# Sixteen row sums of layer 2's gate moved from beside layer 2's output projection to beside layer 1's

## The chip, the cores and the metric

One core of one Trainium2 chip. The metric is device time in microseconds (us) of the whole program, the median of several runs. Engines are named as in the profile: PE is TensorE's matmuls (PEld its weight loads), DVE is VectorE, ACT ScalarE, POOL GpSimd, SP SyncE, whose queue (SPq) issues nearly all DMA loads, in order.

## The reference

A two-layer decoder trunk on 512 tokens of width 2048. Layer 1 mixes tokens by retention (8 heads), layer 2 by latent attention. Each layer is modulated by the conditioning vector c:

```python
c_act = jax.nn.silu(c)
for i in range(DEPTH):
    mod = (c_act @ ada_w[i] + ada_b[i])[:, None, :]
    shift, scale, gate = jnp.split(mod, 3, axis=-1)
    h = rmsnorm(x, norm_g[i]) * (1.0 + scale) + shift
    ...                       # y = retention_branch(h, ...) or mla_branch(h, ...)
    x = x + gate * y
return rmsnorm(x, final_norm_g)
```

All is float32. `ada_w[i]` is 2048 x 6144, so shift, scale and gate have 2048 values each, and each value is a dot product of one row of the transposed matrix with silu(c), 2048 long. The gate of layer 2 is used only where layer 2's output projection is added to x.

## The kernel before

Matrix products run on PE as three passes with a high and a low part of each operand. ACT casts a float32 weight to its high part (L135), DVE subtracts to get the low part (L136); in the trace these are `o_p<-o_r` for layer 1's output projection.

**The row sums.** A modulation piece `(layer, section, part)` is 1024 values: section 0 is the shift, 1 the scale, 2 the gate, part 0 or 1 a half of 2048. The kernel computes a piece as 16 sums: for each of 8 blocks of 128 rows (`b`) and each half `j` of the 2048 products, a load of 128x1024 floats (512 KB, L1165, on SP) and one DVE instruction that multiplies by silu(c) and sums along the row (L1170). When a piece's last sum is through, `use_modulation` adds the halves and the bias: some small DVE operations (L1187 and L253 to L257). 96 such sums, six pieces, run beside layer 1's matmuls, on the list `later_rows`. In the part of layer 1 that matters here the loads' tiles carry the tag `odd0` with two buffers, so a load waits for the sum that used its buffer, two sums before.

**The steps.** Layer 1 is a list of `Step` objects, each one or two units of weights and their matmuls, with pieces of retention put beside them. A step has a count `rows`. At the end of step i, as many row loads as step i+1 has rows are issued on SP; their sums are written in step i+1, behind its other DVE work (`fetched`, `use_ended`). Within an engine the program's order is the order of execution.

**Layer 1's output projection** is four rounds, n = 0 to 3, one for each pair of heads; each of the rounds 0 to 2 has 16 steps: four columns of 512 outputs (`r`), and four units of weights in each (L1472 loads a unit, L1486 is its product, 24 matmuls of 128x512). Between two columns the sums in PSUM are copied out, and the next column's banks are seeded with earlier sums (L1437 and L1434, ACT). Beside round n the retention of heads 2n+2 and 2n+3 is computed, the even head from step 0, the odd one from step 4: rotation of q and k, scores, split of the values (`split_v`), values (y, L158 to L160), group norm (L1320 to L1332), gate (L1338), transposes (L1345). The last round has 8 such steps and then others. In the trace rounds 0, 1 and 2 lie at about 997 to 1109, 1109 to 1222 and 1222 to 1334 us, the last part up to about 1430 us. `light` says how many rows each step of a block has:

```python
light(block, (0, 0, 2, 3, 4, 6, 6, 7, 9, 9, 11, 11, 12, 13, 13, 15))
```

so step 13 of each of the three rounds has two rows.

**The gate of layer 2.** Its first half (part 0) is summed in layer 2's attention steps, two sums a step (`gate_load`, `gate_sum`). Its second half is summed beside layer 2's output projection (L2450, about 1925 us to the end): `o2_hooks(i)` is called at each of its units, and from i = 5 on it issues one load and writes the sum of the load before.

Of the kernel before, what the change touches and what calls it, by code (L numbers as in the profile page):

```python
# [9 lines left out]
F32 = mybir.dt.float32  # L10
# [6 lines left out]
P = 128  # L17
T = 512
NT = T // P
D = 2048  # L20
# [29 lines left out]
def hybrid_trunk_kernel(  # L50
# [32 lines left out]
    base = ctx.enter_context(tc.tile_pool(name="base", bufs=1))  # L83
# [11 lines left out]
    def big(name, dt=F32R):  # L95
        return base.tile([P, 2, T], dt, tag="big", bufs=16, name=name)
# [16 lines left out]
    def small(name, n=1):  # L113
        return base.tile([P, n], F32, tag="small", bufs=24, name=name)
# [135 lines left out]
    def modulate(i, ps_shift, ps_scale, k0, n):  # L250

        if ps_shift is not None:
            DVE.tensor_add(b_col[i][:, k0 : k0 + n], ps_shift, bias_c[i][:, k0 : k0 + n])  # L253
        if ps_scale is not None:
            s = small(f"mod{i}_{k0}", n)
            DVE.tensor_add(s, ps_scale, bias_c[i][:, KD + k0 : KD + k0 + n])
            return DVE.scalar_tensor_tensor(  # L257
                out=a_col[i][:, k0 : k0 + n], in0=s, scalar=1.0,
                in1=norm_c[i][:, k0 : k0 + n], op0=ALU.add, op1=ALU.mult,
            )  # L260
# [199 lines left out]
    A_, V_, T_, S_ = (getattr(mybir.EngineType, e) for e in ("Activation", "DVE", "PE", "SP"))  # L460

    @contextmanager
    def behind(*engines):

        with ExitStack() as stack:
            for e in engines:
                ins = next((i for i in reversed(nc.cur_bb.bb.instructions) if i.engine == e), None)
                if ins is not None:
                    stack.enter_context(tc.issue_after(ins))
            yield  # L470

    def queued(fn, *args):
        with behind(A_, V_, T_, S_):
            return fn(*args)
# [664 lines left out]
    for h in range(1, RH):  # L1139
        if h == 1:  # L1140
# [4 lines left out]
                sums=lambda u: {0: 2, 1: 3, 2: 4, 4: 5, 5: 6, 6: 7}.get(u),  # L1145
# [3 lines left out]
        steps += heads_steps(h)  # L1149


    row_pieces = [(0, 2, 0), (0, 2, 1), (1, 0, 0), (1, 0, 1), (1, 1, 0), (1, 1, 1)]
    later_rows = [(piece, b, j) for piece in row_pieces for b in range(8) for j in range(2)]
    row_sums, ended = {}, []

# [29 lines left out]
    def use_modulation(i, sect, part, mc):  # L1185
        both = small(f"mod_{i}_{sect}_{part}_s", 8)
        DVE.tensor_add(both, mc[:, 0, :], mc[:, 1, :])  # L1187
        if sect == 2:
            cols = slice(part * 8, part * 8 + 8)
            DVE.tensor_add(gate_c[i][:, cols], both, gate_bias[i][:, cols])  # L1190
        else:
            modulate(i, both if sect == 0 else None, both if sect == 1 else None, part * 8, 8)
# [205 lines left out]
    def light(block, which):  # L1398

        for i in which:  # L1400
            block[i].rows += 1

    block = []
# [113 lines left out]
    def go_on(n, r, after):  # L1517

        def done(t):
            if after is None:  # L1520
                o1_banks[n + 1, r, t] = o1_banks[n, r, t]
                return
            keep_sums(n, r, t)
            seed(n, after, t)

        return done

    for n in range(3):
        block = []
        cols = range(4) if n % 2 == 0 else range(3, -1, -1)  # L1530
        for r, after in zip(cols, [*cols[1:], None]):
            block += round_steps(n, r, go_on(n, r, after))
        heads += [retention(2 * n + 2 + i, big) for i in range(2)]
        light(block, (0, 0, 2, 3, 4, 6, 6, 7, 9, 9, 11, 11, 12, 13, 13, 15))
        steps += block


# [1 line left out]
    def outs(r, blocks, half=None):  # L1539

        late = None
        for b in blocks:
            add = x1_out(r, b, half)
            if late is not None:
                late()
            late = add
        late()

    block = round_steps(3, 3, lambda b: None) + round_steps(3, 2, lambda b: None)
    light(block, (0, 0, 2, 2, 4, 5, 6, 6))  # L1550
    block[3].follow = lambda: outs(3, range(4))

    def second_out():
# [169 lines left out]
    def l2_tile(tag, bufs, name, shape=(P, T), dt=F32):  # L1723
        return pools["l2"].tile(list(shape), dt, tag=tag, bufs=bufs, name=name)
# [412 lines left out]


    gate_c_half = {}
    gate_sums = [base.tile([P, 2, 8], F32, tag="mod_c", bufs=2, name=f"gate_sums{i}") for i in range(2)]  # L2140

    def gate_load(part, n):

        j, b = n // 8, n % 8
        if b == 0:
            half = gate_c_half[j] = big(f"c_gate{part}{j}", F32)
            nc.sync.dma_start(
                half.rearrange("p a n -> p (a n)"),
                c_d[0:1, j * 1024 : (j + 1) * 1024].rearrange("o n -> (o n)").partition_broadcast(P),
            )  # L2150
        aw = l2_tile("bw", 2, f"mod_gate_{part}{b}{j}", (P, 2, T))
        r0 = 2 * D + (8 * part + b) * P
        nc.sync.dma_start(aw, ada_t[1, r0 : r0 + P, j * 1024 : (j + 1) * 1024].rearrange("p (a n) -> p a n", a=2))
        return aw, part, j, b, gate_c_half[j]

    def gate_sum(aw, part, j, b, c_half):
        DVE.scalar_tensor_tensor(
            out=aw, in0=aw, scalar=1.0, in1=c_half, op0=ALU.mult, op1=ALU.mult,
            accum_out=gate_sums[part][:, j, b : b + 1],
        )  # L2160
        if (j, b) == (1, 7):
            use_modulation(1, 2, part, gate_sums[part])

    def attention_step(pr):

        nx = pr + 1
        here = [attend(2 * pr + s) for s in range(2)] if pr >= 0 else ()
        both = heads2[nx] = {}
        units_ahead()
        with behind(S_):  # L2170
            sums = [gate_load(0, 2 * nx + i) for i in range(2)]
        if here:
            (sc0, ex0, no0, tr0, sp0, lg0, va0, re0), (sc1, ex1, no1, tr1, sp1, lg1, va1, re1) = here
            queued(lg0)
            queued(lg1)
        low = next_unit("ukv")
        if here:
            for i in range(NT):
                queued(sc0, i)
            for i in range(NT):  # L2180
                queued(ex0, i)
        low()
        if here:
            no0()
        queued(uq_products, nx, 2)
        if here:
            for i in range(NT):
                queued(sc1, i)
            for i in range(NT):
                queued(ex1, i)  # L2190
        t1 = queued(rope_own, both["uq", 2], f"qr_{nx}")
        low = next_unit("ukv") if here else lambda: None
        if here:
            no1()
        low()
        for b in range(2):
            queued(uq_products, nx, b)
        sw = queued(rope_swap, both["uq", 2], f"qr_{nx}")
        low = queued(part_pair, nx, "uq", 0)
        queued(rope_turn, t1, sw)  # L2200
        queued(low)
        low = queued(part_pair, nx, "uq", 1)
        if here:
            queued(tr0)
        queued(low)
        lows = [queued(sp0, j) for j in range(3)] if here else []
        both["qr"] = big(f"qr_{nx}")
        queued(rope_highs, t1, both["qr"])
        for low in lows:
            queued(low)  # L2210
        queued(rope_lows, t1, both["qr"])
        for b in range(2):
            queued(uk_products, nx, b)
            low = queued(part_pair, nx, "uk", b)
            low_w = next_unit("uq")
            queued(low)
            low_w()
        if here:
            queued(va0)
            queued(re0)  # L2220
            queued(tr1)
            for low in [queued(sp1, j) for j in range(3)]:
                queued(low)
        for j in range(2):
            queued(uv_products, nx, j, (1,))
        for j in range(2):
            queued(uv_products, nx, j, (0, 2, 3))
            queued(gate_sum, *sums[j])
            queued(queued(part_values, nx, j))
        if here:  # L2230
            queued(va1)
            queued(re1)
# [130 lines left out]
    o2_in, o2_res = {}, {}  # L2363
    N_ENDS = 5

    gate_pending, gate_n = [], [0, 0]

    def o2_hooks(i):
        l2_hooks.get(i, lambda: None)()
        with behind(V_):  # L2370
            while gate_pending:
                gate_sum(*gate_pending.pop())
        with behind(S_):
            for _ in range(min(1, 16 - gate_n[0]) if 4 < i and i > gate_n[1] else 0):
                gate_pending.insert(0, gate_load(1, gate_n[0]))
                gate_n[0] += 1
        gate_n[1] = i

    def o2_parts(r, u):
        if u not in o2_in:  # L2380
# [235 lines left out]
```

## Time and profile before

| | |
|---|---|
| time, 3 runs | 2119.68, 2119.76 and 2120.03 us, median 2119.76 |
| span of the profiled execution | 2118.4 us |
| mean granted clock of PE | 0.999 |
| busy share of PE, DVE, ACT, POOL | 99%, 79%, 50%, 5% |
| bytes moved | 462.95 MB, 219 GB/s |
| sums of L1170 in layer 1's output projection | x56, 1219 ns busy each, 15.3 us of DVE idle ahead of them for their loads |

The execution that was profiled has a span 1.4 us below the median time. Rows of a timeline begin with the start in us from the start of the span, then the duration, the engine, the line, the operation and its tiles (output <- inputs); in brackets stands how long the engine was idle before and for whom it waited. A row of waits reads: the engine that waited, its tile and line, for whom, then us in total, the number of times and the longest. A matmul's duration overlaps that of the next; from start to start it is about 0.23 us for 128x512.

### The profile page before, as it was taken

What the parts mean: (1) busy time and instruction counts of PE and PEld (TensorE: products, weight loads), DVE (VectorE), ACT (ScalarE), POOL (GpSimd) and SP (SyncE); (2) the same over time, 40 slices, a digit from 0 to 9 for tenths busy, and PEclk for the clock granted to TensorE, in tenths of its full rate; (3) what the DMA queues carried; (4) which work ended last, traced back from release to release, by engine and by line L of the source; (5) the groups of instructions that cost most, each with busy time, mean ns of one, the idle gap of its engine ahead of it and who ended that gap; (6) DMA issues with size and microseconds to landing.
All of it is one profiled execution on the core that took longest, in us unless ns stands there. A gap on an engine that the chain in (4) does not pass through costs nothing.

```text
span 2118.4 us, 30062 instructions
## 1 busy us (share of the span) xinstructions
PE 2104.0 (99%) x11124; PEld 1812.6 (86%) x11124; DVE 1676.0 (79%) x2506; ACT 1055.5 (50%) x1622; POOL 103.6 (5%) x176
## 2 busy tenths in 40 slices
PE   8999999999999999999999999999999999999998
PEld 6888898989889888888888888898889989888888
DVE  7899888888888789666777778768978788886665
ACT  6765444444454444434344444345446575664443
POOL 1001010000000000000000000010001000000000
PEclk9999999999999999999999999999999999999999
DMA  9975786868787778856657556753566644346643
GB/s 381 406 280 195 248 276 222 283 211 272 239 263 250 242 229 283 265 172 196 222 173 241 201 198 230 258 191 108 164 189 209 190 129 149 118 137 219 222 142 138
DMA packets 230101, 462.95 MB, mean 219 GB/s; under 512 B 20881, under 2 KB 84401, under 8 KB 226369
## 3 DMA queue, kind: packets, MB, share of 16 engines
q1 hardware_dynamic: 217312, 421.07, 60.3%
q0 software_dynamic: 11920, 38.91, 4.7%
q8 instruction: 87, 1.43, 0.3%
q10 hardware_dynamic: 722, 1.06, 0.2%
q14 instruction: 60, 0.49, 0.1%
HBM read 417.96 MB, written 43.00 MB: 218 GB/s over the span
## 4 chain that ended last, share of the span: by engine, by line
PE 96%; DMA 1%; DVE 1%; ACT 0%; issue 0%; SPq 0%; DVEq 0%
PE o L1486 16%; PE o L2450 4%; PE x L884 2%; PE x L883 2%; PE x L885 2%; PE y L885 2%; PE y L884 2%; PE s L885 2%; PE s L884 2%; PE s L883 2%; PE y L883 2%; PE uv L2046 2%; PE qk L158 2%; PE s_qk L984 2%; PE x_qk L984 2%; PE qk L160 2%
## 5 line engine op out<-in xcount | busy, mean ns | idle before, releaser
L1486 PE MATMUL o<-o_h,o_p 128*128 128x512 f32 (+1 forms) x1088 | 323.0, 378 | 0.0
L1486 PEld LDWEIGHTS o<-o_h,o_p 128*128 128x128 f32 x1088 | 200.2, 188 | 37.1
L1486 PE MATMUL o<-o_l,o_p 128*128 128x512 f32 (+1 forms) x544 | 204.8, 376 | 0.0
L136 DVE TENSOR_TENSOR o_p<-o_r,o_p 128x1024 fp32r<-128x1024 f32 x64 | 78.1, 1222 | 54.3 <-ACT o_p L135 54.1
L1486 PEld LDWEIGHTS o<-o_l,o_p 128*128 128x128 f32 x544 | 102.3, 188 | 18.3
L2450 PE MATMUL o<-o_h,o_w 128*128 128x512 f32 (+1 forms) x336 | 82.7, 337 | 0.0
L1170 DVE SCALAR_TENSOR_TENSOR mod<-mod,c_odd 128x1024 f32<-128x1024 f32 x56 | 67.2, 1219 | 15.3 <-DMA mod<-in_ada_t_dram 15.3
L135 ACT CAST o_p<-o_r 128x1024 fp32r<-128x1024 f32 x64 | 66.7, 1054 | 22.4 <-PE o L1486 13.3
L158 PE MATMUL qk<-hT,qk_p 128*128 128x512 f32 x192 | 75.0, 391 | 0.0
L160 PE MATMUL qk<-hT,qk_p 128*128 128x512 f32 x192 | 74.9, 390 | 0.0
L389 DVE SCALAR_TENSOR_TENSOR aw<-aw,c_all 128x2048 f32<-128x2048 f32 (+1 forms) x37 | 73.2, 1997 | 2.1 <-DMA aw<-in_ada_t_dram 2.1
L159 PE MATMUL qk<-hT,qk_p 128*128 128x512 f32 x192 | 74.7, 389 | 0.0
L2450 PEld LDWEIGHTS o<-o_h,o_w 128*128 128x128 f32 x336 | 57.7, 188 | 6.9
L2450 PE MATMUL o<-o_l,o_w 128*128 128x512 f32 (+1 forms) x168 | 56.5, 337 | 0.0
L136 DVE TENSOR_TENSOR o_l<-o_in,o_h 128x1024 fp32r<-128x1024 f32 x24 | 29.3, 1222 | 34.2 <-ACT o_h L135 34.2
L1332 ACT ACTIVATE yn<-y,nmr,gn_r 128x512 f32<-128x512 f32 x32 | 22.3, 778 | 67.7 <-DVE nmr L1326 67.7
L135 ACT CAST o_h<-o_in 128x1024 fp32r<-128x1024 f32 x24 | 25.3, 1052 | 61.6 <-PE o L159 40.5
L158 PE MATMUL o<-o_h,o_w 128*128 128x512 f32 x128 | 50.1, 391 | 0.0
L160 PE MATMUL o<-o_h,o_w 128*128 128x512 f32 x128 | 49.8, 389 | 0.0
L159 PE MATMUL o<-o_l,o_w 128*128 128x512 f32 x128 | 49.8, 389 | 0.0
L1170 DVE SCALAR_TENSOR_TENSOR mod<-mod,c_bm 128x1024 f32<-128x1024 f32 x40 | 48.7, 1219 | 0.0
L448 PE MATMUL g<-hT,g_p 128*128 128x512 f32 x192 | 46.1, 389 | 0.0
(1532 smaller groups left out, 6238.3 us busy)
## 6 DMA issues: line engine op xcount, KB each, us to landing
mod<-in_ada_t_dram SPq DMA_DIRECT2D x96, 512.0 KB, 5.7
o_r<-in_ret_w_out_dram SPq DMA_DIRECT2D x64, 512.0 KB, 5.5
aw<-in_ada_t_dram SPq DMA_DIRECT2D x28, 1024.0 KB, 9.5
mod_gate<-in_ada_t_dram SPq DMA_DIRECT2D x32, 512.0 KB, 4.4
o_w_raw<-in_mla_w_out_dram SPq DMA_DIRECT2D x32, 512.0 KB, 4.4
qk_r<-in_ret_w_in_dram SPq DMA_DIRECT2D x48, 256.0 KB, 3.5
qk_r<-qk_d SPq DMA_DIRECT2D x32, 256.0 KB, 6.1
v_r<-v_d SPq DMA_DIRECT2D x32, 256.0 KB, 5.7
```

The lines of the kernel that those rows point to most:

```text
L135: ACT.copy(hi, src)
L136: DVE.tensor_sub(lo, src, hi.bitcast(F32))
L158: PE.matmul(o, lhs[0], rhs[0], start=first and not seeded, stop=False, skip_group_check=seeded)
L159: PE.matmul(o, lhs[0], rhs[1], start=False, stop=False, skip_group_check=seeded)
L160: return PE.matmul(o, lhs[1], rhs[0], start=False, stop=last, skip_group_check=seeded)
L883: PE.matmul(banks[b], a[0], w[0], start=first, stop=False, skip_group_check=True)
L884: PE.matmul(banks[b], a[0], w[1], start=False, stop=False, skip_group_check=True)
L885: PE.matmul(banks[b], a[1], w[0], start=False, stop=True, skip_group_check=True)
L984: PE.matmul(o, w[wp][:, i, b * P : (b + 1) * P], a[ap], start=first and i + b + k == 0, stop=k == 2, skip_group_check=True,)
L1170: DVE.scalar_tensor_tensor(out=aw, in0=aw, scalar=1.0, in1=silu_c[j], op0=ALU.mult, op1=ALU.mult, accum_out=row_sums[piece][:, j, b : b + 1],)
L1486: PE.matmul(o, w[i][:, ki, c0 + b * P : c0 + (b + 1) * P], a[j], start=first and i + j == 0, stop=last and i == 1, skip_group_check=True,)
L2450: PE.matmul(banks2[b][:, cols], w[0][i][:, 0, b * P : (b + 1) * P], o2_moving(w, u, cols)[j], start=u + i + j == 0, stop=u == KD - 1 and i ...
```

## The change

A seventh piece, `(1, 2, 1)`, the second half of layer 2's gate, is added to the list of pieces that are summed beside layer 1, and the steps of layer 1's output projection get 16 rows more: 4 in round 0, 5 in round 1, 6 in round 2, one in the last part. The loads and sums beside layer 2's output projection are taken out, and with them the two broadcast loads of silu(c) for that half (`c_gate10`, `c_gate11`). Since the list is worked through in order, each piece is finished some steps earlier than before, and its small operations move with it.

```diff
-    row_pieces = [(0, 2, 0), (0, 2, 1), (1, 0, 0), (1, 0, 1), (1, 1, 0), (1, 1, 1)]
+    row_pieces = [(0, 2, 0), (0, 2, 1), (1, 0, 0), (1, 0, 1), (1, 1, 0), (1, 1, 1), (1, 2, 1)]
...
+    more_rows = ((3, 8, 8, 13), (3, 4, 8, 9, 13), (2, 5, 8, 8, 10, 13))
     for n in range(3):
...
-        light(block, (0, 0, 2, 3, 4, 6, 6, 7, 9, 9, 11, 11, 12, 13, 13, 15))
+        light(block, (0, 0, 2, 3, 4, 6, 6, 7, 9, 9, 11, 11, 12, 13, 13, 15) + more_rows[n])
...
-    light(block, (0, 0, 2, 2, 4, 5, 6, 6))
+    light(block, (0, 0, 2, 2, 4, 5, 6, 6, 7))
...
-        if (j, b) == (1, 7):
-            use_modulation(1, 2, part, gate_sums[part])
+        if (j, b) == (1, 7):
+            use_modulation(1, 2, 0, gate_sums)
...
     def o2_hooks(i):
         l2_hooks.get(i, lambda: None)()
-        with behind(V_):
-            while gate_pending:
-                gate_sum(*gate_pending.pop())
-        with behind(S_):
-            for _ in range(min(1, 16 - gate_n[0]) if 4 < i and i > gate_n[1] else 0):
-                gate_pending.insert(0, gate_load(1, gate_n[0]))
-                gate_n[0] += 1
-        gate_n[1] = i
```

What it does to the order of instructions is shown at three places, with the rows of before first. A tile `mod_1_1_0_61` is the load for layer index 1, section 1, part 0, block 6, half 1; numbers at the end of names only tell tiles apart.

DVE in step 13 of round 1, from the last split of head 5's values (`v_5_3`) to the first statistics of that head (`st_5_0`); `o1_1_0_3_p` is the weight for round 1's last unit:

```order
L136 TENSOR_TENSOR v_5_3_10555<-v3_5_r_10448,v_5_3_10555 128x512
L1170 SCALAR_TENSOR_TENSOR mod_1_1_0_21_10517,mod_1_1_0_c_10201<-mod_1_1_0_21_10517,c_odd11_8729 128x1024
L1170 SCALAR_TENSOR_TENSOR mod_1_1_0_30_10519,mod_1_1_0_c_10201<-mod_1_1_0_30_10519,c_odd10_8728 128x1024
L136 TENSOR_TENSOR o1_1_0_3_p_10620<-o1_1_0_3_r_10440,o1_1_0_3_p_10620 128x1024
L1320 BN_STATS st_5_0_10624<-y_5_0_10582 128x6
L1321 BN_AGGR bn_5_10623<-st_5_0_10624 128x2
```

and after the change:

```order
L136 TENSOR_TENSOR v_5_3_10580<-v3_5_r_10471,v_5_3_10580 128x512
L1170 SCALAR_TENSOR_TENSOR mod_1_1_0_61_10540,mod_1_1_0_c_9893<-mod_1_1_0_61_10540,c_odd11_8728 128x1024
L1170 SCALAR_TENSOR_TENSOR mod_1_1_0_70_10542,mod_1_1_0_c_9893<-mod_1_1_0_70_10542,c_odd10_8727 128x1024
L1170 SCALAR_TENSOR_TENSOR mod_1_1_0_71_10544,mod_1_1_0_c_9893<-mod_1_1_0_71_10544,c_odd11_8728 128x1024
L136 TENSOR_TENSOR o1_1_0_3_p_10646<-o1_1_0_3_r_10463,o1_1_0_3_p_10646 128x1024
L1320 BN_STATS st_5_0_10650<-y_5_0_10607 128x6
```

Two sums stood ahead of the weight's split, now there are three.

SP for the same step, from the last load of head 5's values (`v3_5_r`) on; `o1_2_0_0_r` is the weight of round 2's first unit, `sg_5` the gate tiles of head 5:

```order
L1255 DMA v3_5_r_10448<-v_d_64 128x512
L1165 DMA mod_1_1_0_21_10517<-in_ada_t_dram 128x1024
L1165 DMA mod_1_1_0_30_10519<-in_ada_t_dram 128x1024
L1472 DMA o1_2_0_0_r_10521<-in_ret_w_out_dram 128x2x512
L1272 DMA sg_5_0_10523<-g_d_65 128x512
```

and after the change:

```order
L1255 DMA v3_5_r_10471<-v_d_64 128x512
L1165 DMA mod_1_1_0_61_10540<-in_ada_t_dram 128x1024
L1165 DMA mod_1_1_0_70_10542<-in_ada_t_dram 128x1024
L1165 DMA mod_1_1_0_71_10544<-in_ada_t_dram 128x1024
L1472 DMA o1_2_0_0_r_10546<-in_ret_w_out_dram 128x2x512
L1272 DMA sg_5_0_10548<-g_d_65 128x512
```

Three loads of rows, into two buffers, now stand ahead of the weight and the gate tiles.

DVE in round 0, from the last split of head 3's rotated keys in step 8 (`qk_3_1_0p`) to the splits of head 2's values:

```order
L136 TENSOR_TENSOR qk_3_1_0p_9186<-rope_3_1_0_t0_9187,qk_3_1_0p_9186 128x512
L1187 TENSOR_TENSOR mod_1_0_0_s_9218<-mod_1_0_0_c_7113 128x8
L253 TENSOR_TENSOR b_col1_92<-mod_1_0_0_s_9218,vcol_84 128x8
L136 TENSOR_TENSOR v_2_0_9236<-v0_2_r_9156,v_2_0_9236 128x512
L136 TENSOR_TENSOR o1_0_2_2_p_9239<-o1_0_2_2_r_9116,o1_0_2_2_p_9239 128x1024
```

and after the change:

```order
L136 TENSOR_TENSOR qk_3_1_0p_9196<-rope_3_1_0_t0_9197,qk_3_1_0p_9196 128x512
L1170 SCALAR_TENSOR_TENSOR mod_1_0_1_01_9152,mod_1_0_1_c_9116<-mod_1_0_1_01_9152,c_odd11_8728 128x1024
L1170 SCALAR_TENSOR_TENSOR mod_1_0_1_10_9154,mod_1_0_1_c_9116<-mod_1_0_1_10_9154,c_odd10_8727 128x1024
L136 TENSOR_TENSOR v_2_0_9244<-v0_2_r_9166,v_2_0_9244 128x512
L136 TENSOR_TENSOR o1_0_2_2_p_9247<-o1_0_2_2_r_9119,o1_0_2_2_p_9247 128x1024
```

Two sums of 128x1024 have taken the place of two operations of 128x8 ahead of the values' first split.

More of the change, by code (lines that the diff above doesn't have):

```diff
@@ L2139, in hybrid_trunk_kernel, with gate_load @@
     gate_c_half = {}
-    gate_sums = [base.tile([P, 2, 8], F32, tag="mod_c", bufs=2, name=f"gate_sums{i}") for i in range(2)]
-    def gate_load(part, n):
+    gate_sums = base.tile([P, 2, 8], F32, tag="mod_c", bufs=2, name="gate_sums")
+    def gate_load(n):
         j, b = n // 8, n % 8
         if b == 0:
-            half = gate_c_half[j] = big(f"c_gate{part}{j}", F32)
+            half = gate_c_half[j] = big(f"c_gate{j}", F32)
             nc.sync.dma_start(
@@ L2150, in gate_load, with gate_sum @@
             )
-        aw = l2_tile("bw", 2, f"mod_gate_{part}{b}{j}", (P, 2, T))
-        r0 = 2 * D + (8 * part + b) * P
+        aw = l2_tile("bw", 2, f"mod_gate_{b}{j}", (P, 2, T))
+        r0 = 2 * D + b * P
         nc.sync.dma_start(aw, ada_t[1, r0 : r0 + P, j * 1024 : (j + 1) * 1024].rearrange("p (a n) -> p a n", a=2))
-        return aw, part, j, b, gate_c_half[j]
-    def gate_sum(aw, part, j, b, c_half):
+        return aw, j, b, gate_c_half[j]
+    def gate_sum(aw, j, b, c_half):
         DVE.scalar_tensor_tensor(
             out=aw, in0=aw, scalar=1.0, in1=c_half, op0=ALU.mult, op1=ALU.mult,
-            accum_out=gate_sums[part][:, j, b : b + 1],
+            accum_out=gate_sums[:, j, b : b + 1],
         )
         if (j, b) == (1, 7):
-            use_modulation(1, 2, part, gate_sums[part])
+            use_modulation(1, 2, 0, gate_sums)
     def attention_step(pr):
@@ L2170, in attention_step @@
         with behind(S_):
-            sums = [gate_load(0, 2 * nx + i) for i in range(2)]
+            sums = [gate_load(2 * nx + i) for i in range(2)]
         if here:
@@ L2364, in hybrid_trunk_kernel @@
     N_ENDS = 5
-    gate_pending, gate_n = [], [0, 0]
     def o2_hooks(i):
         l2_hooks.get(i, lambda: None)()
-        with behind(V_):
-            while gate_pending:
-                gate_sum(*gate_pending.pop())
-        with behind(S_):
-            for _ in range(min(1, 16 - gate_n[0]) if 4 < i and i > gate_n[1] else 0):
-                gate_pending.insert(0, gate_load(1, gate_n[0]))
-                gate_n[0] += 1
-        gate_n[1] = i
     def o2_parts(r, u):
```

## The prediction

> **What bounds the kernel now.** I read the page's first two parts, then the list of waits on TensorE alone, then busy time by stage, then the timelines of VectorE (DVE), ScalarE (ACT), SyncE (SP) and TensorE (PE) around the steps to which rows are added.
>
> ```profile
> PE 2104.0 (99%) x11124; PEld 1812.6 (86%) x11124; DVE 1676.0 (79%) x2506; ACT 1055.5 (50%) x1622; POOL 103.6 (5%) x176
> ```
> ```profile
> core 0: 2118.4 us, clock 0.999
> ```
>
> TensorE bounds nearly everything: 99% of the span, at a mean granted clock of 0.999. The profiled execution's span of 2118.4 us lies 1.4 us under the median of 2119.76; I add what I find to the median.
>
> Everything for which TensorE waited, and then the one wait that belongs to the sums:
>
> ```profile
> PE c_ps L474 <- DMA c_all<-in_c_dram: 3.2, 1, 3.2
> PE xT_ps L474 <- DVE x_diag L571: 2.2, 3, 1.2
> PE v L448 <- DVE hT L423: 0.9, 1, 0.9
> PE y L158 <- DVE o_l L1366: 0.3, 1, 0.3
> PE x_sums L2483 <- ACT x_sq L2422: 0.2, 1, 0.2
> ```
> ```profile
> DVE mod L1170 <- DMA mod<-in_ada_t_dram: 15.3, 7, 2.8
> ```
>
> So nothing but the matmuls limits the stages that the change touches; a gain must come from the small waits, and a loss appears wherever DVE work gets later than TensorE's slack. The last row says that the row sums already arrive at their data early seven times (2.2 us each on average). Beside layer 2's output projection (columns: PE, weight load, DVE, ACT, POOL busy, granted clock, share of DMA, GB/s):
>
> ```profile
> 997.00:1109.00 112.00, 112.00 (x527) 93.97 (x526) 85.39 (x143) 46.21 (x70) 2.98 (x4) 1.00 0.61 209
> ...
> 1925.00:2095.00 170.00, 170.00 (x850) 144.78 (x849) 105.36 (x140) 76.08 (x103) 1.80 (x3) 1.00 0.53 175
> ```
>
> The stage that loses its sums is 170.00 of 170 us busy on TensorE. DVE there is 62% busy, against 76% (85.39 of 112) in the first round of layer 1's output projection, which receives them.
>
> **What is removed.** Sixteen sums, 16 loads of 512 KB and two broadcast loads beside layer 2's output projection: no wait of TensorE in that list belongs to them, and the stage has no idle time. I put the gain at 0.3 us (the last row of the first list, 0.2 us, and gaps too short to be listed), between 0 and 0.5 us (the last two rows together).
>
> **What is added: 16 sums.** There are two tiles for the loads, so the load of a sum waits for the end of the sum two before it. That is the price of every step with three rows: its third load cannot be issued before the first sum of the same step has ended. What this takes I read from two places where a sum already waits for its load; the first row of each pair is the sum two before, the second the sum that waited:
>
> ```profile
> 1108.75 1.22 DVE L1170 SCALAR_TENSOR_TENSOR mod<-mod,c_odd 128x1024 f32<-128x1024 f32 x1
> ...
> 1115.06 1.23 DVE L1170 SCALAR_TENSOR_TENSOR mod<-mod,c_odd 128x1024 f32<-128x1024 f32 x1 [2.81 <-DMA mod<-in_ada_t_dram]
> ...
> 1222.97 1.21 DVE L1170 SCALAR_TENSOR_TENSOR mod<-mod,c_odd 128x1024 f32<-128x1024 f32 x1
> ...
> 1228.25 1.23 DVE L1170 SCALAR_TENSOR_TENSOR mod<-mod,c_odd 128x1024 f32<-128x1024 f32 x1 [1.77 <-DMA mod<-in_ada_t_dram]
> ```
>
> Start to start 6.31 and 5.28 us; I take 5.85, near the middle.
>
> **Step 13 of each round.** Behind the sums stand a split of a weight, the statistics of the odd head, then (ACT) the normalization, the cast of the weight for the next column's first step, and (DVE) that weight's low part, which TensorE uses in the third matmul of that step. In round 1:
>
> ```profile
> 1207.40 1.22 DVE L1170 SCALAR_TENSOR_TENSOR mod<-mod,c_odd 128x1024 f32<-128x1024 f32 x1
> ...
> 1208.55 1.22 DVE L1170 SCALAR_TENSOR_TENSOR mod<-mod,c_odd 128x1024 f32<-128x1024 f32 x1
> ...
> 1209.69 1.22 DVE L136 TENSOR_TENSOR o_p<-o_r,o_p 128x1024 fp32r<-128x1024 f32 x1
> ...
> 1219.42 1.23 DVE L136 TENSOR_TENSOR o_p<-o_r,o_p 128x1024 fp32r<-128x1024 f32 x1 [3.79 <-ACT o_p L135]
> ...
> 1222.07 0.62 PE L1486 MATMUL o<-o_h,o_p 128*128 128x512 f32 x2
> ```
>
> Two sums take 2.29 us here (1207.40 to 1209.69), 1.145 each. With a third, the weight split at 1209.69 would start 5.85 + 1.145 = 7.0 us after the first sum instead: 4.7 us late (4.1 to 5.2 by the two pairs above).
>
> The low part ends at 1220.65, 1.43 us ahead of its use at 1222.07. Every link from 1209.69 to 1219.42 waits for the one before it (the 3.79 us are DVE waiting for ACT), so the delay passes whole: 4.7 - 1.4 = 3.3 us of TensorE idle. The same weight in rounds 0 and 2:
>
> ```profile
> 1105.20 1.23 DVE L136 TENSOR_TENSOR o_p<-o_r,o_p 128x1024 fp32r<-128x1024 f32 x1 [3.79 <-ACT o_p L135]
> ...
> 1109.39 0.61 PE L1486 MATMUL o<-o_h,o_p 128*128 128x512 f32 x2
> ...
> 1330.71 1.23 DVE L136 TENSOR_TENSOR o_p<-o_r,o_p 128x1024 fp32r<-128x1024 f32 x1 [3.79 <-ACT o_p L135]
> ...
> 1334.24 0.62 PE L1486 MATMUL o<-o_h,o_p 128*128 128x512 f32 x2
> ```
>
> Slack 1109.39 - 1106.43 = 3.0 and 1334.24 - 1331.94 = 2.3: stalls of 1.7 and 2.4 us.
>
> **Step 9 of round 1** gets a third row as well. Behind it stand the even head's statistics and normalization on ACT, and behind these ACT's copies that seed the banks of the next column:
>
> ```profile
> 1187.96 1.15 ACT L1434 COPY o<-x 128x512 f32<-128x512 f32 x2
> ...
> 1190.53 0.45 PE L1486 MATMUL o<-o_h,o_p 128*128 128x512 f32 x1
> ...
> 1196.04 1.91 PE L1345 MATMUL yT<-ident,yn 128*128 128x128 f32 x16
> ...
> 1196.95 0.28 DVE L1293 TENSOR_TENSOR s_3f<-s,dec 128x128 f32<-128x128 f32 x1
> ```
>
> The first seed ends near 1188.59, 1.93 us ahead of the matmul at 1190.53; then the transposes need the bank of the scores that DVE reads at 1196.95 to 1197.22, and the last four of the sixteen start near 1197.35: 0.1 us of slack. Here DVE's delay is used up almost whole, first 2.8 us and then 1.8: 4.6 us.
>
> **Step 8 of each round** gets two, one and two rows. Their sums stand on DVE right ahead of the splits of the head's values, which TensorE multiplies next (rounds 0, 1, 2):
>
> ```profile
> 1057.65 0.68 DVE L136 TENSOR_TENSOR v<-v_r,v 128x512 fp32r<-128x512 f32 x1
> ...
> 1058.67 0.39 PE L159 MATMUL y<-v,sT 128*128 128x512 f32 x1
> ...
> 1168.42 0.69 DVE L136 TENSOR_TENSOR v<-v_r,v 128x512 fp32r<-128x512 f32 x1
> ...
> 1169.18 0.49 PE L159 MATMUL y<-v,sT 128*128 128x512 f32 x1
> ...
> 1281.31 0.69 DVE L136 TENSOR_TENSOR v<-v_r,v 128x512 fp32r<-128x512 f32 x1
> ...
> 1282.09 0.46 PE L159 MATMUL y<-v,sT 128*128 128x512 f32 x1
> ```
>
> Slack 0.34, 0.07 and 0.09 us. The short operations on the finished piece that stood there (0.28, 0.28 and 0.48 us) go elsewhere. Added: 2 x 1.145 - 0.28 = 2.0, 0.87 and 1.81; stalls of 1.7, 0.8 and 1.7 us, 4.2 together.
>
> **The other added rows.** The delay that TensorE's idle time has not absorbed runs on: in round 1 about 2.4 us reach step 4's pair of rows, and the split for step 6 comes some 3.0 us late, with 1143.84 - 1141.74 = 2.1 us to spare:
>
> ```profile
> 1140.52 1.22 DVE L136 TENSOR_TENSOR o_p<-o_r,o_p 128x1024 fp32r<-128x1024 f32 x1
> ...
> 1143.84 0.61 PE L1486 MATMUL o<-o_h,o_p 128*128 128x512 f32 x2
> ```
>
> That gives 0.9 us. Round 2 has 4.7 - 3.3 = 1.4 us left over and one row in step 2: with the same slack 0.4 to 1.2, I take 0.8. Round 0's step 3 and round 2's step 10 have a sum beside DVE idle time of the kind bracketed above (3.79 us waiting for ACT): nothing; were that cover gone, 1.145 us each. The last block's row and the short operations moved to round 2's step 11: 0.3 us each, between 0 and 1.
>
> Loads behind a blocked third load on SP's queue. The weight of round 2's first step is issued at 1199.48; another load that waits for the first sum's end goes out at 1208.66, and the weight would follow it:
>
> ```profile
> 1199.48 0.39 SPq L1472 DMA_DIRECT2D o_r<-in_ret_w_out_dram  x1
> ...
> 1208.66 0.33 SPq L1165 DMA_DIRECT2D mod<-in_ada_t_dram  x1
> ```
> ```profile
> 1218.33 2.01 ACT L135 CAST o_p<-o_r 128x1024 fp32r<-128x1024 f32 x2
> ```
> ```profile
> o_r<-in_ret_w_out_dram SPq DMA_DIRECT2D x64, 512.0 KB, 5.5
> ```
>
> With 5.5 us to land it is there at about 1214.5, 3.8 us ahead of its cast, and the cast itself moves back. I cost this at nothing; rival (c) is its other end.
>
> **Sum:** step 13: 1.7 + 3.3 + 2.4 = 7.4; step 9: 4.6; step 8: 4.2; the rest 0.9 + 0.8 + 0.6 = 2.3; less 0.3: 18.2 us. 2119.8 + 18.2 = 2138 us. With 4.1 us for the delay and no carry it is 18.2 - 4 x 0.6 - 2.3 = 13.5; with 5.2 us and all bounds at their high ends, 18.2 + 4 x 0.5 + 3.5 = 23.7.
>
> **The rivals.**
> (a) *Not slower.* The added sums hide in DVE's idle time, and the freed DVE and DMA time beside layer 2's output projection gives back the rest. For it: DVE is idle for 24% of the receiving round, 26.6 us, where some 5 more sums take 6 us; and 16 sums of 1.145 us, 18 us of DVE, go from the other stage. Against it: that idle time lies behind ACT, not ahead of TensorE's needs, and the other stage has no idle time of TensorE to give back, unless its busy time hides gaps. It decides if the third load lands within 2.29 us of the first sum's start (shortest seen: 5.28) and the value splits have some 2 us of slack that the trace doesn't show. Time: 2119.3 to 2120. Chance 0.08 for within 0.2% (4.2 us, about what a measurement tells from no change) and 0.03 for faster than that, which would need the 170 us shortened by 2.5%.
> (b) *Only the step-8 rows cost*, because the third load is quick or the chain behind it has more slack than I read: 2119.8 + 4.2 + 2 = 2126. Chance 0.12.
> (c) *More than the sum.* Loads behind the blocked one come late: if at each of the four three-row places half a landing (2.7 us) comes on top, 4 x 2.7 = 10.8: 2149. For it: the weight goes out 9 us later than now; against it: the 3.8 us left. Chance 0.10.
> (d) *The clock drops in the new stalls.* The trace's mean is 0.999 although TensorE has one listed wait of 3.2 us; the largest stall forecast is 3.3 us. If the clock fell to half for as long as the stall that caused it, the two long stalls (3.3 and 4.6 us, the second in two parts) would cost about half as much again, 4 us: 2142. Chance 0.05. The Trainium skill ("TensorE: Matmul & The Clock Gate", Part 1) says that a whole idle window of 3413 ns halves the clock, and that the window runs free of the program; by that rule a 3.3 us stall just escapes and a 4 us one may not, and no row of this trace tests it.
> (e) *The rows don't move as the change says*: ruled out by the written order, in which three sums stand together.
>
> My forecast keeps 0.62. Slower by over 0.2%: 0.62 + 0.12 + 0.10 + 0.05 = 0.89; within: 0.08; faster: 0.03. The range runs from (b), 2126, to short of (c), 2147.
>
> **What would show it.** In the changed profile: waits of TensorE in 997 to 1430 us of about 18 us, on o_p (L1486 <- DVE L136), on v (L159) and on yT or the seeds; "DVE mod L1170 <- DMA mod" grown from 15.3 us by about 3.5 us at each of four places; the stretch of layer 2's output projection as long as before. It is wrong if TensorE shows no wait for o_p at the starts of rounds 1 and 2, if the sum behind a third load starts within 4 us of the first, or if the granted clock falls.

## The result and the profile after

The changed kernel takes 2142.34 us (median; 2141.55 to 2144.06) against 2119.9 us before (2119.68 to 2120.16): ratio 1.0108, 95% interval 1.0094 to 1.0122, slower by 22.4 us. Forecast were 2138 us, 18.2 us more. The profiled execution, 2141.55 us, has a span of 2139.4 us, 21.0 us longer than the span before.

First the page's busy times, TensorE's longest waits, and DVE's wait for row loads, as shown of before (the waits: total us, times, longest):

```profile
PE 2108.4 (99%) x11124; PEld 1811.2 (85%) x11124; DVE 1676.3 (78%) x2506; ACT 1054.1 (49%) x1622; POOL 103.3 (5%) x176
```
```profile
PE o L1486 <- ACT o_p L135: 5.1, 3, 1.8
PE o L1486 <- DVE o_p L136: 4.4, 6, 1.0
PE xT_ps L474 <- DVE x_diag L571: 3.5, 3, 2.5
PE c_ps L474 <- DMA c_all<-in_c_dram: 2.5, 1, 2.5
PE yT L1345 <- DVE s_3f L1293: 1.9, 3, 0.8
PE y L159 <- DVE v L136: 1.6, 2, 1.1
PE s L158 <- ACT yn L1332: 1.4, 1, 1.4
PE y L158 <- ACT v L135: 0.8, 1, 0.8
PE y L158 <- DVE o_l L1366: 0.7, 1, 0.7
```
```profile
DVE mod L1170 <- DMA mod<-in_ada_t_dram: 34.5, 15, 3.9
```

Six of these nine waits were not in the list before (`xT_ps` and `c_ps` belong to the start of the kernel, and `o_l` stood there with 0.3 us). Among them are the ones named in the prediction: the weight of a column's first step (`o_p`), the head's values (`v`), the transposes (`yT`). DVE now waits 34.5 us for row loads instead of 15.3, 15 times instead of 7, and the work of DVE is the same.

By stage (columns as before), the first rows for the kernel before, the others after the change, each from the first matmul of a round on:

```profile
1109.00:1222.00 113.00, 112.67 (x527) 93.97 (x526) 85.14 (x143) 51.79 (x81) 2.02 (x2) 1.00 0.61 210
1222.00:1334.00 112.00, 112.00 (x525) 93.57 (x524) 87.14 (x147) 51.49 (x80) 2.02 (x2) 1.00 0.63 214
```
```profile
997.00:1112.00 115.00, 112.44 (x525) 93.50 (x523) 86.23 (x145) 45.25 (x70) 2.78 (x4) 1.00 0.65 221
1112.00:1235.00 123.00, 114.98 (x525) 93.57 (x526) 92.96 (x158) 51.53 (x81) 2.01 (x2) 1.00 0.62 214
1235.00:1354.00 119.00, 113.34 (x524) 93.11 (x522) 92.67 (x157) 50.83 (x81) 2.01 (x2) 1.00 0.66 228
...
1946.00:2116.00 170.00, 170.00 (x849) 144.77 (x848) 87.19 (x107) 76.03 (x103) 1.68 (x3) 1.00 0.36 119
```

The rounds are 3, 10 and 7 us longer. Some 16 of these 20 us are idle time of TensorE (8.0 us in round 1: 123.00 less 114.98); the other 4 stand as longer busy time, 2108.4 us against 2104.0 in all. Beside layer 2's output projection DVE's busy time falls from 105.36 to 87.19 us and the traffic from 175 to 119 GB/s, and TensorE is as busy as before: 170.00 of 170 us.

Step 13 of round 1 after the change, on DVE:

```profile
1218.55 1.22 DVE L1170 SCALAR_TENSOR_TENSOR mod<-mod,c_odd 128x1024 f32<-128x1024 f32 x1
...
1219.70 1.22 DVE L1170 SCALAR_TENSOR_TENSOR mod<-mod,c_odd 128x1024 f32<-128x1024 f32 x1
...
1223.94 1.23 DVE L1170 SCALAR_TENSOR_TENSOR mod<-mod,c_odd 128x1024 f32<-128x1024 f32 x1 [3.01 <-DMA mod<-in_ada_t_dram]
...
1225.09 1.22 DVE L136 TENSOR_TENSOR o_p<-o_r,o_p 128x1024 fp32r<-128x1024 f32 x1
...
1234.66 1.23 DVE L136 TENSOR_TENSOR o_p<-o_r,o_p 128x1024 fp32r<-128x1024 f32 x1 [3.31 <-ACT o_p L135]
```

and on SP and TensorE:

```profile
1219.81 0.33 SPq L1165 DMA_DIRECT2D mod<-in_ada_t_dram  x1
```
```profile
1234.68 0.50 PE L1486 MATMUL o<-o_h,o_p 128*128 128x512 f32 x1 [1.76 <-ACT o_p L135]
...
1235.94 0.73 PE L1486 MATMUL o<-o_h,o_p 128*128 128x512 f32 x2 [0.53 <-DVE o_p L136]
```

The third load goes out at 1219.81, right behind the first sum's end near 1219.77. Its sum starts 5.4 us after the first one, DVE stands still for 3.0 us of them, and the weight's split begins 6.54 us after the first sum instead of 2.29. TensorE then waits for the cast (1.76 us) and for the low part (0.53 us).

Where the time went, by the lengths of the steps (first L1486 matmul of a step to that of the next, after less before; the small changes left out). A stall shows where TensorE waits, one to four steps behind the added rows: for step 13 in step 15 and the next round's step 0, for step 8 in steps 9 and 12, for step 9 in steps 11, 12 and 13:

```
place                             forecast   step lengths after less before
step 13, round 0                   1.7       1.81 + 0.96
step 13, round 1                   3.3       1.92 + 0.94
step 13, round 2                   2.4       1.88 + 0.94
step 9, round 1                    4.6       3.51 + 1.87 + 0.34
step 8, rounds 0, 1, 2             4.2       0.85 + 0.66, 0.21, 2.25 + 0.80
carried into rounds 1 and 2        1.7       1.18, 0.11 + 1.30
other rows, less the gain          0.3       -
sum                               18.2       21.5
```

The 0.34 us in step 13 of round 1 can't be put down to the change: in the profile of before without (below), which changes nothing there, the same step is 0.64 us shorter than in the kernel before.

### The profile page after: what moved, and what is told of

Its sections match the earlier page's. It is cut to its first block, busy times and chain, and to the rows that moved or that the text cites. A ratio compares the mean times of both kernels' runs of the same rounds, so it can differ in the third digit from the quotient of the medians.

```text
span 2139.4 us, 30059 instructions
## 1 busy us (share of the span) xinstructions
PE 2108.4 (99%) x11124; PEld 1811.2 (85%) x11124; DVE 1676.3 (78%) x2506; ACT 1054.1 (49%) x1622; POOL 103.3 (5%) x176
## 4 chain that ended last, share of the span: by engine, by line
PE 84%; DVE 7%; DMA 5%; ACT 2%; issue 2%; SPq 0%; POOL 0%; DVEq 0%; ACTq 0%; POOLq 0%
PE o L1486 7%; PE o L2441 4%; PE x L883 2%; PE x L884 2%; PE y L883 2%; PE s L883 2%; PE x L885 2%; PE y L885 2%; PE s L885 2%; PE s L884 2%; PE y L884 2%; DMA mod<-in_ada_t_dram 2%; PE uv L2047 2%; PE qk L158 2%; PE s_qk L984 2%; PE x_qk L984 2%
## 5 line engine op out<-in xcount | busy, mean ns | idle before, releaser
L1486 PE MATMUL o<-o_h,o_p 128*128 128x512 f32 (+1 forms) x1088 | 324.6, 379 | 9.9 <-ACT o_p L135 5.1
L1486 PEld LDWEIGHTS o<-o_h,o_p 128*128 128x128 f32 x1088 | 199.6, 188 | 50.7 <-DVE o_p L136 7.2
L1486 PE MATMUL o<-o_l,o_p 128*128 128x512 f32 (+1 forms) x544 | 204.9, 377 | 0.0
L1486 PEld LDWEIGHTS o<-o_l,o_p 128*128 128x128 f32 x544 | 102.3, 188 | 18.2
L1170 DVE SCALAR_TENSOR_TENSOR mod<-mod,c_odd 128x1024 f32<-128x1024 f32 x72 | 86.5, 1219 | 34.5 <-DMA mod<-in_ada_t_dram 34.5
L136 DVE TENSOR_TENSOR o_p<-o_r,o_p 128x1024 fp32r<-128x1024 f32 x64 | 78.0, 1221 | 37.6 <-ACT o_p L135 37.3
L159 PE MATMUL qk<-hT,qk_p 128*128 128x512 f32 x192 | 74.7, 389 | 0.0
L136 DVE TENSOR_TENSOR o_l<-o_in,o_h 128x1024 fp32r<-128x1024 f32 x24 | 29.3, 1222 | 54.5 <-ACT o_h L135 54.5
L159 PE MATMUL o<-o_l,o_w 128*128 128x512 f32 x128 | 49.8, 389 | 0.0
L136 DVE TENSOR_TENSOR o_w<-o_w_raw,o_w 128x1024 fp32r<-128x1024 f32 x32 | 38.9, 1218 | 13.4 <-ACT o_w L135 13.4
```

The costliest lines, as they stand in the source:

```text
L136: DVE.tensor_sub(lo, src, hi.bitcast(F32))
L159: PE.matmul(o, lhs[0], rhs[1], start=False, stop=False, skip_group_check=seeded)
L1170: DVE.scalar_tensor_tensor(out=aw, in0=aw, scalar=1.0, in1=silu_c[j], op0=ALU.mult, op1=ALU.mult, accum_out=row_sums[piece][:, j, b : b + 1],)
L1486: PE.matmul(o, w[i][:, ki, c0 + b * P : c0 + (b + 1) * P], a[j], start=first and i + j == 0, stop=last and i == 1, skip_group_check=True,)
```

## The experiments

The theory: what costs is, above all, the wait of a third row's load for one of two buffers; second, the sums of step 8 right ahead of the values' splits. The rivals: the amount of DVE work, wherever it stands; loads that come late behind a third load on SP.

**No third load.** In the four steps with three rows the third row's load is left out and its sum reads the second row's tile, so four sums are those of other rows.

```diff
-            aw = pool.tile([P, 2, T], F32, tag=tag, bufs=2, name=f"{name}_{b}{j}")
-            nc.sync.dma_start(aw, ...)
+            if not third[0]:          # third[0]: this is a step's third row
+                aw = pool.tile([P, 2, T], F32, tag=tag, bufs=2, name=f"{name}_{b}{j}")
+                nc.sync.dma_start(aw, ...)
...
-            for _ in range(steps[i + 1].rows):
+            for k in range(steps[i + 1].rows):
+                third[0] = k == 2
```

> The changed kernel, but in the four steps with three rows the third row's load is left out: its sum is still made, over the tile of the second row (so four of the modulation sums are those of another row). DVE does the same work; only the wait for a buffer and a load is gone, and with it the load that blocked SP. Theory (the third load can be issued only when the first sum has ended): the stalls of TensorE at steps 13 and 9 go, 13.8 us by the changed kernel's step lengths (1.81 + 0.96, 3.51 + 1.87, 1.92 + 0.94, 1.88 + 0.94), and most of the 2.6 us carried into rounds 1 and 2: 2126 to 2129 us. Rival (the sums themselves are too much for DVE there): no more than 1 us better, 2141 us. Rival (the loads blocked behind the third load come late): also 2126 to 2129, told apart by the kernel in which only the order on SP changes.

Measured: 2128.8 us (2127.85 to 2129.07), ratio to before 1.0041 (1.0026 to 1.0056). 13.5 us are gone with the four loads, while DVE does the same sums. None of TensorE's waits is for ACT's cast of `o_p` any more; four that are left in the rounds:

```profile
PE o L1487 <- DVE o_p L136: 1.6, 2, 0.8
PE y L159 <- DVE v L136: 1.4, 2, 0.9
PE yT L1346 <- DVE s_3f L1294: 1.3, 2, 0.8
PE y L158 <- ACT v L135: 0.9, 1, 0.9
```

The steps behind 13 are back at their old lengths in all three rounds. One part of step 9's price stays: step 12 of round 1 is still 1.87 us longer. DVE work alone makes that one, as the 0.1 us of slack there said.

The expectation also had most of the 2.6 us go that are carried into rounds 1 and 2. That was wrong: 2.2 us of them stay, 1.12 at step 6 of round 1 and 1.12 at step 4 of round 2, which are the two waits for `o_p` above. In round 1, DVE's split of `qk_0p` begins 0.7 us into step 2 in the kernel before and 3.1 us into it in the changed kernel, with the third loads and without them. So what is carried on comes with the third sums themselves, not with the wait for their loads. The profile of this run also has about 1.7 us of low clock, described in the last section.

**Two a step.** The third rows go back beside layer 2's output projection: `more_rows = ((3, 8, 8), (3, 4, 8), (2, 5, 8, 8, 10))`, with the old loop of `o2_hooks` for the four sums that are left.

> The changed kernel without the four third rows: 12 rows stay beside layer 1's output projection, four go back beside layer 2's. Theory: as without the third loads, 2126 to 2129 us, since DVE's 4 x 1.145 us weigh nothing beside the waits for loads. Rival (the amount of DVE work decides, in proportion to the rows): 12/16 of the loss stays, 2137 us.

Measured: 2125.04 us (2124.34 to 2125.99), ratio 1.0026 (1.0016 to 1.0036). It is 1 us better than the expected range: 12 of the 16 rows cost 5.3 us, a quarter of the loss. The rival by amount of work (2137 us) is out. But the four third sums do not weigh nothing, as was expected: they are the difference to the kernel without the third loads, 3.8 us, of which 2.2 are the two waits for `o_p` just named and 1.2 lie in step 12 of round 1 (1.87 us longer there, 0.66 here). So the loss of some 22 us is roughly 13.5 for the four late loads, 3.8 for their sums and 5.3 for the other 12 rows.

**Thirds only.** `more_rows = ((13,), (9, 13), (13,))`, no row in the last part, 12 sums beside layer 2's output projection.

> Only the four third rows (step 13 of rounds 0, 1, 2 and step 9 of round 1) are added beside layer 1's output projection, the other 12 sums stay beside layer 2's. Theory: the 13.8 us of those steps and about 1 us carried on: 2133 to 2136 us. Rival (in proportion to the rows): 4/16 of the loss, 2125 us. Rival (all hides once the steps ahead are not crowded): 2120 to 2122 us.

Measured: 2136.01 us (2134.81 to 2137.97), ratio 1.0076 (1.006 to 1.0093): four rows cost 16.3 us, at the upper end of the theory's range and far from a quarter of the loss.

**Step 8 only.** `more_rows = ((8, 8), (8,), (8, 8))`, 11 sums beside layer 2's.

> Only the five rows of step 8 (two, one and two in rounds 0, 1, 2) are added beside layer 1's output projection, the other 11 sums stay beside layer 2's. Theory (the sums stand right ahead of the values' splits, which have 0.1 to 0.3 us of slack): 4.2 us by the prediction, 0.9 + 0.2 + 2.3 = 3.4 us by the changed kernel's step 9, up to 4.8 us with what its step 12 lost: 2123 to 2125 us. Rival (these rows hide too): 2120 us.

Measured: 2124.11 us (2123.14 to 2125.16), ratio 1.0021 (1.0011 to 1.003): 4.4 us, where the prediction had 4.2. TensorE's waits include `PE y L159 <- DVE v L136: 1.8, 2, 1.2`. With the 16.3 us of the third rows this makes 20.7 of 22.4 us; how the rest divides between the other seven rows and what crowded places carry on isn't settled, and the 16.3 us hold some low clock (below).

**Third behind.** On SP the third load goes behind the weight and the gate tiles:

```diff
-            for _ in range(steps[i + 1].rows):
+            for _ in range(min(2, steps[i + 1].rows)):
...
             for load in step.beside["load"]:
                 load()
+            for _ in range(step.rows - 2):
+                fetched += [(i - 1, f) for f in (next(later, None),) if f is not None]
```

> The changed kernel, but on SP the third row's load is issued behind the next weight and the four gate tiles, so that it blocks none of them; it still waits for the first sum. Theory (what costs is DVE waiting for that load): no change beyond 1 us to either side, 2141 to 2144 us. Rival (the weight and the gate tiles blocked on SP come late): several us better, 2130 to 2137 us.

Measured: 2140.67 us (2138.88 to 2141.37), ratio 1.0098 (1.0084 to 1.0111). DVE waits for row loads as long as in the changed kernel (34.1 us, 15 times), and the time is 1.7 us lower than the changed kernel's, a little below the 2141 us expected; the two ratios' intervals overlap. Its profile has one stretch of low clock (1234.6 to 1238 us, clock 0.50) where the changed kernel's has none; by step lengths, with 1.7 us taken off for it (an estimate, below), it is some 2.7 us shorter. So blocked weights and gate tiles are a small part of what costs, and the rival's several us are out.

**Spread.** All 16 rows beside layer 1's output projection, at steps 1, 3, 5, 10 and 14 of each round and one in the last part.

> All 16 rows beside layer 1's output projection, but at steps 1, 3, 5, 10 and 14 of each round and one in the last part: no step has three rows, step 8 none, step 10 one. Theory (where a row stands decides): 0 to 4 us over the kernel before, 2120 to 2124 us, the rest from rows in steps 3 and 5 whose weight splits have 2.1 to 3.2 us of slack. Rival (16 more sums are too much for this stage wherever they stand): 2135 us or more.

Measured: 2122.03 us (2120.34 to 2123.49), ratio 1.0011 (1.0002 to 1.002). The same sums cost a tenth when no step has three rows and none stands in step 8. DVE still waits 24.1 us for row loads, 11 times, mostly where TensorE does not feel it. The largest part of what is left does not lie behind the rows of steps 3 and 5, as was expected, but in step 9 of round 2, which is 1.48 us longer: ahead of step 8's work DVE waits 4.39 us for a row load (2.38 us at this place in the kernel before), and TensorE gets the head's values late:

```profile
1282.91 0.50 PE L158 MATMUL y<-v,sT 128*128 128x512 f32 x1 [0.67 <-ACT v L135]
1283.71 0.50 PE L159 MATMUL y<-v,sT 128*128 128x512 f32 x1 [0.30 <-DVE v L136]
```

It isn't faster than before.

**Before without.** The kernel before, with the second half's sums and all their loads left out (`for _ in range(0)` in `o2_hooks`; the second half of the gate uses the first half's sums).

> The kernel before with the 16 sums, their loads and the two broadcast loads beside layer 2's output projection left out (the second half of layer 2's gate uses the first half's sums). It shows the most that their removal can bring. Theory: TensorE waits for nothing there: 0 to 0.5 us, 2119.3 to 2119.9 us. Rival (the busy time there hides gaps): 2 us or more, 2118 us or less.

Measured: 2119.66 us (2119.06 to 2120.26), ratio 1.0001 (0.9992 to 1.001). There was nothing to gain from their removal, so no better place for them can beat the kernel before by more than that interval allows.

**Each third row alone**, `more_rows` with a single row, 15 sums beside layer 2's output projection.

> Only the third row of step 13 of round 0 is beside layer 1's output projection; the other 15 sums stay beside layer 2's. By the prediction's working (delay 4.7 us, slack 3.0): 1.7 us; with the 6.0 us that the third sum's load took in the kernel with all four third rows: 1.9 us. 2121.5 us. Rival (alone, the delay hides): 2119.7 us.

> Only the third row of step 9 of round 1. By the prediction's working 4.6 us, by the step lengths of the kernel with all four third rows up to 5.4 us: 2124.3 to 2125.1 us. Rival (the second of its two stalls comes from other added rows): 2.8 us, 2122.5 us.

> Only the third row of step 13 of round 1. By the prediction's working (delay 4.7 us, slack 1.4) 3.3 us: 2123 us. New theory: a stall of this length in some executions makes the granted clock fall to half for a window of 3.4 us, as in three profiles of the experiments before, at a price of 1.7 us: so the single runs lie near 2123 or near 2124.7 us, and the mean clock of the longer ones is lower by 0.001. Rival (the clock does not matter): the runs lie within 1 us, as those of the kernel before do.

> Only the third row of step 13 of round 2. By the prediction's working (delay 4.7 us, slack 2.3) 2.4 us: 2122.1 us; with 6.0 us for the load 2.6 us. By the clock theory some runs 1.7 us longer, fewer than for step 13 of round 1, whose stall is longer. Rival: as there.

Measured, against 2119.53 us for the kernel before:

```
                  forecast   measured   median us (range)               ratio (95%)
round 0 step 13     1.7        1.9      2121.48 (2120.78 to 2123.60)    1.0010 (1.0001, 1.0020)
round 1 step  9     4.6        3.7      2123.21 (2122.64 to 2124.58)    1.0018 (1.0010, 1.0027)
round 1 step 13     3.3        3.6      2123.13 (2121.23 to 2124.58)    1.0017 (1.0009, 1.0026)
round 2 step 13     2.4        3.5      2123.02 (2121.28 to 2124.47)    1.0016 (1.0007, 1.0025)
```

Together 12.7 us; all four in one kernel cost 16.3. Stretches of low clock, each some 3.4 us long, blur this comparison: there is one behind the stall in each profile of a single row of step 13, two in that of thirds only (1233.3 to 1236.7 and 1349.3 to 1352.7 us, clock 0.51 and 0.50), none in step 9's and none in the changed kernel's. With 1.7 us taken off for each (an estimate, below), the step lengths of the single rows are 2.4, 4.1, 2.9 and 2.6 us, 12.0 together as forecast; the same places make 13.8 us in the changed kernel.

Step 9's time lies between the forecast and the rival, and its profile decides: step 12 of round 1 is 1.87 us longer though no other row was added, so the rival is out. What is smaller than forecast is the first stall, 2.25 us.

The clock: the profile of round 2's step 13 alone, by stretches (the column behind POOL is the granted clock):

```profile
1330.00:1337.00 7.00, 4.91 (x21) 3.42 (x20) 2.25 (x4) 5.61 (x7) 0.93 (x1) 1.00 0.38 141
...
1337.40:1340.80 3.40, 3.40 (x10) 2.63 (x9) 3.40 (x6) 0.00 (x0) 0.00 (x0) 0.53 0.05 5
1340.80:1345.00 4.20, 4.20 (x28) 3.67 (x28) 2.28 (x4) 1.41 (x3) 0.00 (x0) 1.00 0.83 248
```
```profile
1334.93 0.50 PE L1488 MATMUL o<-o_h,o_p 128*128 128x512 f32 x1 [1.57 <-ACT o_p L135]
...
1336.19 0.73 PE L1488 MATMUL o<-o_h,o_p 128*128 128x512 f32 x2 [0.52 <-DVE o_p L136]
...
1338.07 1.05 PE L1488 MATMUL o<-o_h,o_p 128*128 128x512 f32 x2
1338.92 0.63 PE L1488 MATMUL o<-o_l,o_p 128*128 128x512 f32 x1
1339.35 1.05 PE L1488 MATMUL o<-o_h,o_p 128*128 128x512 f32 x2
```

After two waits of 1.57 and 0.52 us the clock is near half for about 3.4 us: three matmuls take 1.28 us from start to start (1338.07 to 1339.35) where they took 0.68. At half speed 3.4 us cost 1.7 us, an estimate. For round 2's step 13 the single runs bear this out: five runs with a mean clock of 0.999 lie at 2121.28 to 2122.67 us, six with 0.998 at 2123.02 to 2124.47, 1.6 us apart on average. For round 1's step 13 the runs at 0.998 (2122.73, 2123.13, 2124.58) lie among the others, so there the split that I expected doesn't show, though the profile of the run of 2123.13 us has such a stretch (1224.1 to 1227.5 us, clock 0.50). Six of eleven runs in round 2 and three in round 1 are at 0.998; the other way round was expected.

## Why the prediction came out as it did

The direction, the places and the main mechanism, the late third load, were right; the size was 4 us short (18.2 forecast, 22.4 measured), and some terms fitted better in number than in cause.

- **What is removed: 0.3 us.** Right. Leaving the sums out altogether moves the time by less than its uncertainty (ratio 1.0001).
- **The delay of a three-row step.** 5.85 us from the first sum to the third was taken, of 5.28 to 6.31. In the changed kernel it was 5.4 us in the fence above and 5.9 to 6.1 us at the other three places, between the two bounds; DVE waits 3.0 to 3.7 us for each of the four loads, where about 3.5 was forecast. Taking the loads away removed 13.5 us; the forecast for these four places was 12.0 with the third sums' own time on DVE in it.
- **Step 13.** 1.7, 3.3 and 2.4 us forecast; 2.8, 2.9 and 2.8 us in the trace. Round 0's term was too small: the first sum of the step came 0.7 us later in its step than before, as it does in the kernel with the rows of step 8 alone (0.9 us), and the third sum started 6.06 us after it instead of 5.85. I had costed each place against the slack of before, as though the others were not there. Alone, round 0's row costs 1.9 us.
- **Step 9 of round 1.** 4.6 us forecast; 5.4 in the step lengths, 3.7 alone. Its second part, the wait of the transposes, is 1.87 us as forecast (1.8). The first part was put in the wrong place: of the forecast 2.8 us ahead of the seeds only 0.36 us of waiting is found there. TensorE had already waited in step 11, 0.93 us for a weight's low part and 1.44 us ahead of the scores `s`, by the profile for ACT's normalization (`yn`); neither wait was costed:

```profile
1195.06 0.50 PE L158 MATMUL s<-qk_0p,qk_0p 128*128 128x512 f32 x1 [1.44 <-ACT yn L1332]
...
1199.46 0.50 PE L1486 MATMUL o<-o_h,o_p 128*128 128x512 f32 x1 [0.36 <-ACT o L1434]
```

- **Step 8.** 4.2 us forecast, 4.4 us alone, and that they agree is luck. With step 8's rows alone the steps that wait for the values are 0.99, 0.21 and 1.22 us longer, 2.4 together where 4.2 was forecast. The rest lies in step 12 (0.67, 0.63 and 0.58 us), where the transposes wait for the scores' bank; the prediction had this wait behind step 9 only. In the changed kernel the division is as uneven: 2.25 us in round 2 instead of 1.7, 0.2 in round 1 instead of 0.8.
- **Loads behind a blocked load cost nothing.** Nearly right for the third loads (third behind: 1.7 us by the medians, 2.7 by step lengths, against 10.8 for rival (c)), wrong by 0.8 us at step 8 of round 2, a place that I had not costed for this. There a second row waits for a buffer and blocks SP for 6.55 us, the values' loads go out behind it, and ACT waits for them:

```profile
1283.47 6.55 SPq L1165 DMA_DIRECT2D mod<-in_ada_t_dram  x2
1290.11 0.39 SPq L1472 DMA_DIRECT2D o_r<-in_ret_w_out_dram  x1
1290.55 1.91 SPq L1255 DMA_DIRECT2D v_r<-v_d  x4
```
```profile
1297.32 0.62 ACT L135 CAST v<-v_r 128x512 fp32r<-128x512 f32 x1 [0.73 <-DMA v_r<-v_d]
```

- **Carried on: 1.7 us.** 2.6 us in the trace (1.18 in round 1, 1.41 in round 2): the term of round 2 was the small one, 0.8. The cause was wrong as well: the prediction carried on the delay of the third load, and without that load 2.2 us stay.
- **Rival (d), the clock**, had a chance of 0.05 and was tied to stalls of 3.3 us and more. It happens, after shorter stalls than that, but not in the profiled execution of the changed kernel, whose span is 21.0 us longer with no stretch of low clock in layer 1's output projection. Its runs lie 2.5 us apart where those before lie 0.5 apart. The mean clock of the other three is 0.998, 0.998 and 0.997, against 0.999 in the profiled execution and before. That fits such windows in them; no profile of those runs was taken, so it is not shown.

The step that fell short most is the sum itself: places were added up almost as if independent, each with the slack of the undisturbed trace. Alone, the third rows make 12.0 us by step lengths and the rows of step 8 make 4.4, close to the 12.0 and 4.2 forecast; together with what is carried on they make 21.5. The difference between the 21.5 us and the measured 22.4 stays open, with the clock as its likeliest cause.

## What to carry to other kernels

Work that is moved into a step with idle time on its engine is paid for by what stands behind it in that engine's order: read the slack of the next consumer, not the idle share. With two load buffers the third load of a burst waits for the first consumer and then for its whole landing. Here the same 16 rows, spread so that no step has three and none stands ahead of an urgent split, cost 2.3 us instead of 22.4; with the third rows alone sent back, the other 12 cost 5.3. Before moving work away from a stage, leave it out there once: if that gains nothing, there is nothing for another place to win.

## What the runs showed of the hardware

TensorE's clock can drop after much less idle time than I expected. In the profiles of two a step and no third load, 3.4 us near half clock began 0.2 and 0.6 us after two short waits for `v`, at the same place (step 9 of round 2). The waits in two a step, and the clock of that stretch in two a step and in no third load:

```profile
1284.13 1.20 PE L158 MATMUL y<-v,sT 128*128 128x512 f32 x4 [0.79 <-ACT v L135]
1286.06 0.57 PE L159 MATMUL y<-v,sT 128*128 128x512 f32 x1 [0.74 <-DVE v L136]
```
```profile
1286.30:1289.70 3.40, 3.40 (x9) 2.65 (x9) 3.40 (x6) 0.29 (x1) 0.00 (x0) 0.51 0.85 272
```
```profile
1290.90:1294.30 3.40, 3.40 (x10) 2.61 (x9) 3.40 (x6) 0.00 (x0) 0.00 (x0) 0.51 0.61 192
```

1.5 us of waits in all, no single one above 0.8 us, were enough in the first of these; in the changed kernel's profile 1.76 and 0.53 us were not, nor 1.4 us and more at step 9 of round 1. At the start of round 1, 1.42 and 0.53 us were enough with the row of round 0 alone (1111.8 to 1115.2 us, clock 0.53), and 1.64 and 0.53 us were not in the changed kernel. So the length of the waits alone doesn't decide. The Trainium skill ("TensorE: Matmul & The Clock Gate", Part 1) has a window of 3413 ns that runs free of the program; the length agrees with these stretches, and a window whose position varies would explain why the same stall is punished in some executions only, which no run here tests. The Trainium skill's table there also has the clock at half after at least one idle window of about 3.4 us. That does not agree: the traces show the drop after 1.5 to 3.0 us of waits (0.79 and 0.74 in two a step, 2.47 and 0.52 in thirds only).
